# First mixer of a two-block transformer: matrices of a pair of heads kept compactly instead of as blocks on a diagonal

## The chip, the cores and the metric

The kernel runs on one core of a Trainium2 chip. The metric is device time in microseconds (us), the median of several runs. The five engines are TensorE (PE in the profile, with its weight loads as PEld), VectorE (DVE), ScalarE (ACT), GpSimd (POOL) and SyncE (SP), whose queue issues nearly all DMA.

## The reference

Two transformer blocks on 256 tokens of width 1024, batch 1. The change lies in the RWKV half of the first block's mixer: 8 heads of 64, a recurrence over the tokens with a state of 64x64 for each head.

```python
def step(state, inp):
    r_t, k_t, v_t, w_t, a_t, b_t = inp
    sa = jnp.einsum('bhvk,bhk->bhv', state, a_t)
    state = state * w_t[:, :, None, :] + sa[..., None] * b_t[:, :, None, :] + v_t[..., None] * k_t[:, :, None, :]
    return state, jnp.einsum('bhvk,bhk->bhv', state, r_t)
...
ret = jax.nn.silu(rp[..., 3 * RET_WIDTH:]) * ret.reshape(B, S, RET_WIDTH)
rw = rwkv7_time_mix(proj[..., 4 * RET_WIDTH:], rwkv_mu[l], ...)
mixed = jnp.concatenate([ret, rw], axis=-1).astype(x.dtype)
h = h + mixed @ w_out[l]
h = h + hier_moe(rms_norm(h, norm2_gain[l]), ...)
```

After the mixer follow 32 experts of which each token uses two, then a second block (attention and a large product-key layer).

## The kernel before

The first mixer is a set of Python generators (features, four pairs of heads in `rwkv`, retention, output projection) that `interleave` runs by turns while the program is built: each `yield` names a number, the TensorE time that is to pass before the generator goes on. The sum of that time is kept in `self.pe` (`mm` adds an estimate for every product, `tr` a fixed one). So the order of every engine's instructions is fixed when the program is built, and each engine works its own list in that order.

`rwkv(p, ...)` treats heads 2p and 2p+1 together, on partitions 0 to 63 and 64 to 127, with the 256 tokens in 4 chunks of 64. For each chunk it builds a 64x64 triangular matrix (`NB[:, :, 0]`, a unit matrix with the products of `bbd` and `ar` above it), and inverts it in five levels of doubling: `X` holds the inverse so far and `XT` its transpose. A level is a block of products NB·X, an operation on VectorE that masks it into `Z`, and a block of products Z·XT and XT·Z, from which `X` and `XT` are copied again. Then come `UU` (inverse times right-hand sides), `G` and `Q`, and a chain over the chunks whose state is `Sb`.

Every matrix that serves as the stationary operand is kept as [128, ..., 128] with the two heads as blocks on a diagonal and zeros elsewhere. So a product for one head runs over all 128 rows and writes 64 columns (`128*64` in the profile), the two heads' products follow each other, and whatever writes such a matrix needs one operation for each head:

```python
for h in range(2):
    nc.vector.tensor_tensor(Z[col(h), :, col(h)], b[col(h)],
                            mlev[col(h), k][:, None, :].to_broadcast([64, 4, 64]), OP.mult)
```

The products of the features and of the output projection (`u,xt`, `xt,u`, `u,mix` in the profile) use weights split into two parts by ScalarE (L214) and VectorE (L221); their blocks stand between the small ones. The expert stage reads 192 chunks of 1 MB (`in_wB`) into places that are reused: SyncE issues a load when the products on the old content are done, the first ones into memory that the mixer gives up (`first_experts`, `prefetch`, L911).

Of the kernel before, what the change touches and what calls it, by code (L numbers as in the profile page):

```python
# [21 lines left out]
S, D = 256, 1024  # L22
# [8 lines left out]
def shape_constants():  # L31
    f = np.float32
    p = np.arange(128)
    q = p % 64
    c64 = np.arange(64)
    parts = {}
# [4 lines left out]
    lv = []  # L41
    for k in range(6):
        b = 1 << k
        t, s = q[:, None], c64[None, :]
# [10 lines left out]
    n = 0  # L55
# [17 lines left out]
    t = np.arange(S, dtype=np.float64)  # L73
# [92 lines left out]
class K:  # L166
# [375 lines left out]
    def rwkv_setup(self):  # L542
        nc = self.nc
        zs = {}
        E = lambda shape, tag, dt=F32, **k: self.t(self.ap["first"], shape, dt, tag, **k)
        for tag, shape, n in (("sg", [128, 4, 65], 2), ("tl", [128, 2, S], 1), ("bbd", [128, 4, 128], 1), ("kbd", [128, 4, 128], 1),
                              ("NB", [128, 4, 2, 128], 2), ("nka", [128, 4, 128], 1), ("nkr", [128, 4, 128], 2),
                              ("Z", [128, 4, 128], 2), ("Sb", [128, 3, 128], 2)):
            zs[tag] = [self.t(self.ap["even" if tag == "Z" else ("even", "odd")[j] if tag in ("NB", "nkr", "Sb") else "first"], shape, F32, f"{tag}_{j}_") for j in range(n)]
            for z in zs[tag]:  # L550
                nc.gpsimd.memset(z, 0.0)
        zs["tl"] = zs["tl"][0]
        zs["gs"] = E([128, S], "gs")
        zs["h0"] = E([128, 8], "h0")
        o, _ = VEC["rwkv_w0"]
        nc.vector.tensor_scalar(zs["h0"], self.vec[:, o:o + 8], 0.5, None, op0=OP.mult)
        zs["fe"] = [E([128, 257], f"fe_{b}_") for b in range(2)]
        for f in zs["fe"]:
            nc.vector.memset(f[:, 0:1], 0.0)
        zs["smask"] = E([128, 4, 65], "smask")  # L560
        nc.gpsimd.memset(zs["smask"], 1.0)
        nc.gpsimd.memset(zs["smask"][:, :, 0:1], 0.0)
        for z in zs["NB"]:
            nc.gpsimd.tensor_copy(z[:, :, 0], self.ident[:, None, :].to_broadcast([128, 4, 128]))
        return zs

    def rwkv(self, p, zs, lora, gup):

        nc = self.nc
# [5 lines left out]
        ones2, ident, ident2 = self.c("ones2"), self.ident, self.c("ident2")  # L575
# [7 lines left out]
        sg, bbd, kbd, NB, nka, nkr, Z, Sb = (zs[k][p % len(zs[k])] for k in ("sg", "bbd", "kbd", "NB", "nka", "nkr", "Z", "Sb"))  # L583
# [71 lines left out]
        for src in (bbd, kbd):  # L655
            b = self.bank([128, 4, 2, 64])
            for c in range(4):
                for h in range(2):
                    mm(b[col(h), c].rearrange("p a t -> p (a t)"), src[:, c, col(h)],
                       ar[:, c].rearrange("p a t -> p (a t)"), start=True, stop=True)  # L660
            for h in range(2):
                bc = lambda z: z[:, None, :].to_broadcast([64, 4, 64])
# [10 lines left out]
        for c in range(4):  # L673
            for j, f in enumerate((ar[:, c, 0], w4(vp)[:, c])):
                for h in range(2):
                    mm(b[col(h), j, c], f, ident[:, col(h)], start=True, stop=True)
        nc.scalar.activation(rhs[:, :, 0], b[:, 0], AF.Copy)
        nc.scalar.activation(vt, b[:, 1], AF.Copy)
        bT = T([128, 4, 128], "bT")
        kT = T([128, 4, 128], "kT")  # L680
        for src, dst in ((bbd, bT), (kbd, kT)):
            b = self.bank([128, 4, 128])
# [6 lines left out]
        for c in range(4):  # L689
            for h in range(2):  # L690
                mm(b[col(h), c], nka[:, c, col(h)], vt[:, c], start=True, stop=True)
# [5 lines left out]
        XT = T([128, 4, 128], "XT")  # L697
        nc.gpsimd.tensor_tensor(XT, NB[:, :, 0], mt0[:, None, :].to_broadcast([128, 4, 128]), OP.mult)
        b = self.bank([128, 4, 64])
        for c in range(4):  # L700
            for h in range(2):
                mm(b[col(h), c], NB[:, c, 0, col(h)], ident2, start=True, stop=True)
        nc.vector.tensor_tensor(X, b, mlev[:, 0][:, None, :].to_broadcast([128, 4, 64]), OP.mult)
        for k in range(1, 6):
            yield 1.0
            b = self.bank([128, 4, 64])
            for c in range(4):
                for h in range(2):
                    mm(b[col(h), c], NB[:, c, 0, col(h)], X[:, c], start=True, stop=True)
            for h in range(2):  # L710
                nc.vector.tensor_tensor(Z[col(h), :, col(h)], b[col(h)],
                                        mlev[col(h), k][:, None, :].to_broadcast([64, 4, 64]), OP.mult)
            yield 1.2
            b = self.bank([128, 2, 4, 64])
            for c in range(4):
                for h in range(2):
                    mm(b[col(h), 1, c], Z[:, c, col(h)], XT[:, c, col(h)], start=True, stop=True)
                if k < 5:
                    for h in range(2):
                        mm(b[col(h), 0, c], XT[:, c, col(h)], Z[:, c, col(h)], start=True, stop=True)  # L720
# [9 lines left out]
        for c in range(4):  # L730
            for h in range(2):
                mm(b[col(h), c], XT[:, c, col(h)], rhs[:, c].rearrange("p a t -> p (a t)"), start=True, stop=True)
# [3 lines left out]
        for c in range(4):  # L736
            if c < 3:
                for h in range(2):
                    mm(b[col(h), 0, c], UU[:, c, 0], bT[:, c, col(h)], start=True, stop=True)
            for h in range(2):  # L740
                mm(b[col(h), 1, c], UU[:, c, 0], NB[:, c, 1, col(h)], start=True, stop=True)
# [3 lines left out]
        nc.vector.tensor_tensor(Q, b[:, 1], ar[:, :, 1], OP.add)  # L745
        for c in range(3):
            yield 1.75
            b = self.bank([128, 64])
            terms = [(bT[:, c], UU[:, c, 1], True), (kT[:, c], vt[:, c], True)]
            if c:  # L750
                terms.append((G[:, c], Sb[:, c - 1], False))
            self.col_sums(b, terms)
            for h in range(2):
                nc.vector.tensor_scalar(Sb[col(h), c, col(h)], b[col(h)], gam[col(h), c:c + 1], None, op0=OP.mult)
# [3 lines left out]
        for c in range(4):  # L758
            terms = [(NB[:, c, 1], UU[:, c, 1], True), (nkr[:, c], vt[:, c], True)]
            if c:  # L760
                terms.append((Q[:, c], Sb[:, c - 1], False))
            self.col_sums(b[:, c], terms)
# [14 lines left out]
        for c in range(4):  # L777
            for h in range(2):
                mm(b[col(h), c], y[:, c], ident[:, col(h)], start=True, stop=True)
# [12 lines left out]

    def col_sums(self, out, terms):

        for n, (l, r, left) in enumerate(terms):
            for h in range(2):
                hs = slice(64 * h, 64 * h + 64)
                self.mm(out[hs], l[:, hs] if left else l, r if left else r[:, hs],
                                      start=n == 0, stop=n == len(terms) - 1, skip_group_check=True)
# [1091 lines left out]
```

## Time and profile before

| | |
|---|---|
| median of 3 runs | 1655.43 us (1652.95 to 1655.73) |
| profiled execution, its own time | 1654.47 us |
| its span, first to last instruction | 1652.7 us |
| busy share of TensorE, VectorE, ScalarE, GpSimd | 96%, 60%, 40%, 14% |
| stretch of the RWKV matrices | about 40 to 205 us |
| expert stage, DMA | about 256 to 700 us at 407 GB/s |

Shares over the span are means over very different stages. Matmuls are pipelined: their bars overlap, and idle time of TensorE is counted from the modelled end of the last one.

### The profile page before, as it was taken

The numbers are of one execution on the slowest core, as the hardware profiler recorded it, in microseconds if no ns is written. First come the engines' busy times: TensorE is split into PE (matmuls) and PEld (weight loads), VectorE is DVE, ScalarE is ACT, GpSimd is POOL, SyncE is SP. The second block draws the span as 40 slices with busy tenths as digits, with TensorE's granted clock in tenths as the row PEclk, the third lists the DMA queues.
The fourth block names the chain that finished last, engine by engine and source line by source line (L and its number), as shares of the span: only waits on it lengthen the run. The fifth ranks groups of instructions, "written<-read, shape, count | busy, mean of one in ns | idle before, by whom it ended". The sixth has DMA issues, their size and how long they took to land.

```text
span 1652.7 us, 27958 instructions
## 1 busy us (share of the span) xinstructions
PE 1590.4 (96%) x11022; PEld 1223.9 (74%) x11022; DVE 997.4 (60%) x1917; ACT 658.5 (40%) x1175; POOL 233.2 (14%) x264
## 2 busy tenths in 40 slices
PE   7998999999999998899999999999999999999998
PEld 7787784534443343367889999999999888888887
DVE  6878662212121211288979988788899755555554
ACT  5333341211121111155655456555544444444443
POOL 5212120000000000066110000123445100000000
PEclk9999999999999999999999999999999999999999
DMA  6222688999999999964255556555555566666664
GB/s 202 91 65 65 225 359 348 415 389 419 420 419 420 420 419 420 370 194 136 82 181 174 182 179 193 166 166 166 167 160 163 166 195 195 193 192 193 194 197 155
DMA packets 84296, 390.63 MB, mean 236 GB/s; under 512 B 9632, under 2 KB 9776, under 8 KB 63424
## 3 DMA queue, kind: packets, MB, share of 16 engines
q1 hardware_dynamic: 83088, 384.48, 65.2%
q0 software_dynamic: 928, 3.25, 0.6%
q8 instruction: 89, 1.46, 0.4%
q10 hardware_dynamic: 144, 1.05, 0.2%
q14 instruction: 47, 0.39, 0.1%
HBM read 386.65 MB, written 2.10 MB: 235 GB/s over the span
## 4 chain that ended last, share of the span: by engine, by line
PE 53%; DVE 2%; POOL 2%; issue 1%; ACT 0%; ACTq 0%; DVEq 0%; POOLq 0%
PE b L255 52%; POOL rs_r L341 1%; DVE u L221 1%; PE b L267 1%; DVE g L1748 0%; POOL rs_m L339 0%; POOL y L1439 0%; POOL rs_r L1428 0%; DVE oh L1856 0%; ACT s L1472 0%; DVE h L472 0%; DVE u L1705 0%; DVE ss L1426 0%; DVE qz L1451 0%; DVE mx L1468 0%
## 5 line engine op out<-in xcount | busy, mean ns | idle before, releaser
L214 ACT ACTIVATE u<-u 128x1024 fp32r<-128x1024 f32 x334 | 354.2, 1061 | 387.0 <-PE b L255 363.9
L221 DVE TENSOR_TENSOR u<-u,u 128x1024 fp32r<-128x1024 f32 x334 | 412.9, 1237 | 148.4 <-PE b L255 115.1
L255 PE MATMUL b<-mix,u 128*128 128x256 f32 x3456 | 425.6, 281 | 0.0
L255 PEld LDWEIGHTS b<-mix,u 128*128 128x128 f32 x3456 | 411.1, 188 | 0.0
L255 PE MATMUL b<-u,oh 128*128 128x512 f32 x1536 | 350.3, 390 | 2.0 <-ACT oh L1688 2.0
L255 PEld LDWEIGHTS b<-u,oh 128*128 128x128 f32 x1536 | 289.3, 188 | 62.8 <-ACT oh L1688 2.2
L255 PE MATMUL b<-mr,u 128*64 128x512 f32 x944 | 231.2, 595 | 17.3 <-DMA mr<-in_wB 17.2
L255 PEld LDWEIGHTS b<-mr,u 128*64 128x64 f32 x944 | 74.5, 137 | 157.1 <-issue 119.0
L1151 DVE TENSOR_TENSOR hh<-hh,b 128x512 f32<-128x512 f32 x16 | 11.0, 687 | 230.2 <-PE b L255 230.2
L1732 POOL TENSOR_TENSOR g<-g,gelu 128x4 f32<-128x4 f32 (+43 forms) x87 | 94.3, 1084 | 355.1 <-ACT gelu L1731 348.1
L255 PE MATMUL b<-u,xt 128*128 128x512 f32 x480 | 124.6, 410 | 0.8 <-DVE u L221 0.8
L255 PE MATMUL b<-mr,hT 128*64 128x512 f32 x480 | 117.5, 603 | 5.5 <-DVEq L1215 2.4
L255 PEld LDWEIGHTS b<-u,xt 128*128 128x128 f32 x480 | 89.9, 192 | 21.6 <-DVE u L221 1.1
L1196 DVE SCALAR_TENSOR_TENSOR u<-b,sw,u 128x512 fp32r<-128x512 f32 x32 | 23.9, 750 | 133.3 <-ACT u L1195 133.3
L255 PEld LDWEIGHTS b<-mr,hT 128*64 128x64 f32 x480 | 35.9, 138 | 74.6 <-issue 69.7
L1176 ACT ACTIVATE hT<-b 128x512 f32<-128x512 f32 x16 | 9.6, 597 | 159.6 <-PE b L267 159.6
L1689 DVE TENSOR_TENSOR oh<-g,oh 128x512 fp32r<-128x512 f32 x64 | 44.3, 693 | 41.0 <-ACT oh L1688 40.9
L1324 POOL MEMSET qz<- 128x2048 f32 x2 | 3.5, 1799 | 451.0 <-DVEq L1215 451.0
L1195 ACT ACTIVATE u<-b,sw 128x512 fp32r<-128x512 f32 x32 | 21.9, 687 | 109.0 <-PE b L255 109.0
L1748 DVE TENSOR_TENSOR g<-g,b 128x252 f32<-128x252 f32 (+47 forms) x111 | 61.5, 592 | 0.0
L1856 DVE TENSOR_TENSOR oh<-oh,gw 128x512 f16<-128x512 f16 x128 | 54.4, 464 | 0.0
L255 PE MATMUL b<-xt,u 128*128 128x256 f32 x336 | 47.7, 297 | 3.9 <-DVE u L221 2.3
(390 smaller groups left out, 1736.6 us busy)
## 6 DMA issues: line engine op xcount, KB each, us to landing
mr<-in_wB SPq DMA_DIRECT2D x160, 1024.0 KB, 15.9
u<-in_down SPq DMA_DIRECT2D x128, 512.0 KB, 3.6
u<-in_up SPq DMA_DIRECT2D x128, 512.0 KB, 3.5
mr<-in_wB SPq DMA_DIRECT2D x36, 512.0 KB, 15.0
u<-in_wA SPq DMA_DIRECT2D x30, 512.0 KB, 3.7
u<-in_wB SPq DMA_DIRECT2D x28, 512.0 KB, 13.5
u<-in_wC SPq DMA_DIRECT2D x24, 512.0 KB, 4.4
u<-in_wQ SPq DMA_DIRECT2D x16, 512.0 KB, 3.6
```

Of the source, the lines that this page charges most:

```text
L214: nc.scalar.activation(hi, r, AF.Copy)
L221: nc.vector.tensor_tensor(lo, r, hi.bitcast(F32), OP.subtract)
L255: self.nc.tensor.matmul(out, l, r, start=start, stop=stop, **k)
L267: self.nc.tensor.transpose(out, x, self.ident)
L341: nc.gpsimd.tensor_tensor(r, m, self.mhalf[:, :width], OP.pow)
L1151: nc.vector.tensor_tensor(self.hh, self.hh, bs[1], OP.mult)
L1195: nc.scalar.activation(yh[:, o], b, AF.Copy, scale=sw)
L1196: nc.vector.scalar_tensor_tensor(yl[:, o], b, sw, yh[:, o].bitcast(F32), op0=OP.mult, op1=OP.subtract)
L1689: nc.vector.tensor_tensor(lo, src, hi.bitcast(F32), OP.subtract)
L1732: nc.gpsimd.tensor_tensor(dst[:, 0:n], dst[:, 0:n], g[:, 0:n], OP.mult)
L1748: nc.vector.tensor_tensor(d, d, s, OP.mult)
L1856: self.nc.vector.tensor_tensor(w[:, :, part].rearrange("p t (k x) -> p t k x", x=2), o[:, :, 0].rearrange("p t (k x) -> p t k x", x=2), se ...
```

## The change

`NB`, `nka`, `nkr`, `Z`, `XT`, `Sb` and the former `bbd`, `kbd`, `bT`, `kT` (now `bd`, `kd` and the halves of `bkT`) become [128, ..., 64], a head on 64 partitions. A helper `heads` issues the two products of a pair, each over 64 rows and 64 columns; every write of such a matrix is one operation over 128 partitions. `XT` is copied by ScalarE alone. The transposes of `bbd` and `kbd` (`tr`, 128x128) become products with a 64-row identity. The zeroing of the old matrices by GpSimd goes, and within a level the product that becomes `X` is issued ahead of that which becomes `XT`. Places in memory move, since the tiles are smaller.

```diff
-        for tag, shape, n in (("sg", [128, 4, 65], 2), ("tl", [128, 2, S], 1), ("bbd", [128, 4, 128], 1), ("kbd", [128, 4, 128], 1),
-                              ("NB", [128, 4, 2, 128], 2), ("nka", [128, 4, 128], 1), ("nkr", [128, 4, 128], 2),
-                              ("Z", [128, 4, 128], 2), ("Sb", [128, 3, 128], 2)):
...
+        for tag, shape, n in (("sg", [128, 4, 65], 2), ("tl", [128, 2, S], 1), ("NB", [128, 4, 2, 64], 2)):
...
+        def heads(out, l, r, start=True, stop=True):
+            for h in range(2):
+                mm(out[col(h)], l[col(h)], r[col(h)], start=start, stop=stop, skip_group_check=not (start and stop))
...
-        for h in range(2):
-            nc.vector.tensor_tensor(bbd[col(h), :, col(h)], w4(kr)[col(h)], e3p[col(h)], OP.mult)
-            nc.gpsimd.tensor_tensor(kbd[col(h), :, col(h)], w4(k2)[col(h)], e3p[col(h)], OP.mult)
+        bd, kd = E([128, 4, 64], "bd"), E([128, 4, 64], "kd")
+        nc.vector.tensor_tensor(bd, w4(kr), e3p, OP.mult)
+        nc.gpsimd.tensor_tensor(kd, w4(k2), e3p, OP.mult)
...
-                if src is bbd:
-                    nc.vector.copy_predicated(NB[col(h), :, 0, col(h)], bc(mtri[col(h), 0].bitcast(I32)), b[col(h), :, 0])
-                    nc.vector.tensor_tensor(NB[col(h), :, 1, col(h)], b[col(h), :, 1], bc(mtri[col(h), 1]), OP.mult)
-                else:
-                    nc.vector.tensor_tensor(nka[col(h), :, col(h)], b[col(h), :, 0], bc(mtri[col(h), 0]), OP.mult)
-                    nc.vector.tensor_tensor(nkr[col(h), :, col(h)], b[col(h), :, 1], bc(mtri[col(h), 1]), OP.mult)
+                heads(b[:, c].rearrange("p a t -> p (a t)"), src[:, c], ar[:, c].rearrange("p a t -> p (a t)"))
+            if src is bd:
+                nc.vector.copy_predicated(NB[:, :, 0], bc(0).bitcast(I32), b[:, :, 0])
+                nc.vector.tensor_tensor(NB[:, :, 1], b[:, :, 1], bc(1), OP.mult)
+            else:
+                nc.vector.tensor_tensor(nka, b[:, :, 0], bc(0), OP.mult)
+                nc.vector.tensor_tensor(nkr, b[:, :, 1], bc(1), OP.mult)
...
-                self.tr(b[:, c], src[:, c])
-            nc.scalar.activation(dst, b, AF.Copy)
+                heads(b[:, j, c], src[:, c], ident2)
+        nc.scalar.activation(bkT, b, AF.Copy)
...
-            for h in range(2):
-                nc.vector.tensor_tensor(Z[col(h), :, col(h)], b[col(h)],
-                                        mlev[col(h), k][:, None, :].to_broadcast([64, 4, 64]), OP.mult)
+            nc.vector.tensor_tensor(Z, b, lev(k), OP.mult)
...
-            nc.vector.tensor_copy(XT[col(0), :, col(0)], b[col(0), 1])
-            nc.scalar.activation(XT[col(1), :, col(1)], b[col(1), 1], AF.Copy)
+            nc.scalar.activation(XT, b[:, 1], AF.Copy)
...
-            for h in range(2):
-                nc.vector.tensor_scalar(Sb[col(h), c, col(h)], b[col(h)], gam[col(h), c:c + 1], None, op0=OP.mult)
+            nc.vector.tensor_scalar(Sb[:, c], b, gam[:, c:c + 1], None, op0=OP.mult)
```

What this does to the lists of the engines is seen at three places. The first is VectorE's list at about 45 to 49 us, where the products of `bbd` and `kbd` for the first pair of heads are masked into `NB`, `nka` and `nkr`. Before:

```order
L221 TENSOR_TENSOR u_539<-u_369,u_501 128x1024
L664 COPY_PREDICATED NB_44_222<-cst_80,b_568 64x4x64
L665 TENSOR_TENSOR NB_44_222<-b_568,cst_80 64x4x64
L664 COPY_PREDICATED NB_44_222<-cst_80,b_568 64x4x64
L665 TENSOR_TENSOR NB_44_222<-b_568,cst_80 64x4x64
L667 TENSOR_TENSOR nka_46_226<-b_581,cst_80 64x4x64
L668 TENSOR_TENSOR nkr_47_228<-b_581,cst_80 64x4x64
L667 TENSOR_TENSOR nka_46_226<-b_581,cst_80 64x4x64
L668 TENSOR_TENSOR nkr_47_228<-b_581,cst_80 64x4x64
L528 TENSOR_TENSOR fe_55_243<-b_543,R_280 128x256
```

Now:

```order
L218 TENSOR_TENSOR u_519<-u_349,u_481 128x1024
L663 COPY_PREDICATED NB_42_218<-cst_80,b_550 128x4x64
L664 TENSOR_TENSOR NB_42_218<-b_550,cst_80 128x4x64
L666 TENSOR_TENSOR nka_548<-b_561,cst_80 128x256
L667 TENSOR_TENSOR nkr_549<-b_561,cst_80 128x256
L525 TENSOR_TENSOR fe_46_223<-b_523,R_260 128x256
```

Eight operations on 64 partitions became four on 128; the neighbours are the same. The second place is TensorE's list at about 71 to 73 us, the end of the same step for the second pair, where `cst` is the identity and `X,NB` a level of the first pair. Before:

```order
L255 MATMUL b_918<-cst_72,ft_632 64x64 x2
L267 MATMUL b_939<-cst_72,bbd_42_218 128x128 x4
L267 MATMUL b_945<-cst_72,kbd_43_220 128x128 x4
L255 MATMUL b_951<-X_669,NB_44_222 64x64 x8
L255 MATMUL b_739<-u_634,xt_13_133 128x512
```

Now:

```order
L252 MATMUL b_894<-cst_80,ft_615 64x64 x2
L252 MATMUL b_914<-cst_80,bd_782 64x64 x8
L252 MATMUL b_914<-cst_80,kd_783 64x64 x8
L252 MATMUL b_932<-X_652,NB_42_218 64x64 x8
L252 MATMUL b_722<-u_617,xt_13_133 128x512
```

Eight transposes of 128x128 became sixteen products of 64x64, and nothing stands elsewhere. The third place is VectorE's list at about 121 to 129 us, ahead of a state `Sb` of the second pair for which TensorE waits. Before:

```order
L754 TENSOR_SCALAR Sb_52_237<-b_1567,gam_697 64x64 x2
L528 TENSOR_TENSOR fe_55_243<-b_1458,R_280 128x256
L530 TENSOR_TENSOR d_1575<-fe_55_243 128x256
L532 SCALAR_TENSOR_TENSOR ft_1577<-d_1575,vec_83,fe_55_243 128x256
L221 TENSOR_TENSOR u_1581<-u_1189,u_1452 128x1024
L636 TENSOR_SCALAR ri_1598<-b_1595 128x256
L637 RECIPROCAL ri_1598<-ri_1598 128x256
L640 SCALAR_TENSOR_TENSOR ar_1601<-kr_1539,e_1514 128x4x64
L642 TENSOR_TENSOR ri_1598<-ri_1598,av_1496 128x256
L643 TENSOR_TENSOR kr_1539<-kr_1539,ri_1598 128x256
L645 TENSOR_TENSOR bbd_42_218<-kr_1539,e_1515 64x4x64 x2
L754 TENSOR_SCALAR Sb_52_237<-b_1610,gam_697 64x64 x2
```

Now:

```order
L745 TENSOR_SCALAR Sb_1503<-b_1534,gam_681 128x64
L525 TENSOR_TENSOR fe_46_223<-b_1424,R_260 128x256
L527 TENSOR_TENSOR d_1541<-fe_46_223 128x256
L529 SCALAR_TENSOR_TENSOR ft_1543<-d_1541,vec_83,fe_46_223 128x256
L218 TENSOR_TENSOR u_1547<-u_1164,u_1418 128x1024
L637 TENSOR_SCALAR ri_1564<-b_1561 128x256
L638 RECIPROCAL ri_1564<-ri_1564 128x256
L641 SCALAR_TENSOR_TENSOR ar_1567<-kr_1506,e_1480 128x4x64
L643 TENSOR_TENSOR ri_1564<-ri_1564,av_1462 128x256
L644 TENSOR_TENSOR kr_1506<-kr_1506,ri_1564 128x256
L646 TENSOR_TENSOR bd_1572<-kr_1506,e_1481 128x256
L745 TENSOR_SCALAR Sb_1503<-b_1576,gam_681 128x64
```

The order is the same; the two `Sb` and the `bbd` are each one operation for two.

## Rows read from the trace of the kernel before

**Rows 1.** Busy time by stretch: start:end, length, each engine busy (instructions), clock, DMA.

```profile
40.00:70.00 30.00, 26.50 (x346) 21.97 (x347) 28.57 (x58) 10.50 (x22) 9.45 (x8) 1.00 0.29 90
70.00:112.00 42.00, 38.89 (x636) 34.44 (x632) 29.68 (x65) 13.56 (x26) 6.35 (x8) 0.99 0.24 75
112.00:150.00 38.00, 34.17 (x395) 28.39 (x394) 30.28 (x71) 13.10 (x28) 7.80 (x10) 0.87 0.18 58
150.00:185.00 35.00, 31.71 (x606) 27.06 (x606) 27.74 (x63) 11.43 (x27) 11.23 (x13) 1.00 0.49 175
185.00:256.00 71.00, 70.04 (x540) 58.22 (x538) 47.44 (x99) 27.21 (x40) 14.04 (x25) 1.00 0.80 311
256.00:700.00 444.00, 422.05 (x2031) 180.92 (x2030) 81.95 (x165) 71.52 (x141) 0.00 (x0) 1.00 0.99 407
```

**Rows 2.** Waits of TensorE, 0 to 280 us: total, times, longest.

```profile
PE b L255 <- DVE Z L711: 5.4, 8, 2.5
...
PE b L255 <- DVE Sb L754: 2.5, 1, 2.5
...
PE b L255 <- DVE nka L667: 2.1, 4, 0.9
...
PE b L255 <- DVE X L703: 1.9, 3, 1.0
```

**Rows 3.** VectorE groups by form, 0 to 280 us: busy, mean ns, idle before.

```profile
L711 DVE TENSOR_TENSOR Z<-b,cst 64x256 f32<-64x256 f32 x40 | 16.8, 420 | 2.7 <-PE b L255 1.9
...
L723 DVE COPY XT<-b 64x256 f32<-64x256 f32 x20 | 8.3, 415 | 12.2 <-ACT X L722 11.2 <-PE b L255 0.8
...
L664 DVE COPY_PREDICATED NB<-cst,b 64x256 f32<-64x256 int32 x8 | 3.6, 447 | 0.1
...
L703 DVE TENSOR_TENSOR X<-b,cst 128x256 f32<-128x256 f32 x4 | 1.7, 418 | 0.0
```

**Rows 4.** VectorE in order of time, 104 to 110 us: start, length, [idle before].

```profile
104.86 0.43 DVE L774 TENSOR_TENSOR y<-y,rs_r 128x256 f32<-128x256 f32 x1 [1.45 <-POOL rs_r L341]
...
109.03 0.87 DVE L711 TENSOR_TENSOR Z<-b,cst 64x256 f32<-64x256 f32 x2
```

**Rows 5.** TensorE in order of time, 104 to 110 us.

```profile
109.49 0.33 PE L255 MATMUL b<-XT,Z 128*64 128x64 f32 x2 [2.55 <-DVE Z L711]
```

**Rows 6.** VectorE in order of time, 124 to 130 us.

```profile
124.99 1.75 DVE L637 RECIPROCAL ri<-ri 128x256 f32<-128x256 f32 x1
...
127.92 0.85 DVE L645 TENSOR_TENSOR bbd<-kr,e 64x256 f32<-64x256 f32 x2
...
128.80 0.60 DVE L754 TENSOR_SCALAR Sb<-b,gam 64x64 f32<-64x64 f32 x2
```

**Rows 7.** TensorE in order of time, 71 to 75 us.

```profile
71.56 0.66 PE L267 MATMUL b<-cst,bbd 128*128 128x128 f32 x4
...
72.59 0.69 PE L255 MATMUL b<-X,NB 128*64 128x64 f32 x16
...
73.20 1.66 PE L255 MATMUL b<-u,xt 128*128 128x512 f32 x6
```

**Rows 8.** TensorE in order of time, 129 to 133 us.

```profile
129.86 2.93 PE L255 MATMUL b<-u,xt 128*128 128x512 f32 x6
```

**Rows 9.** TensorE matmuls by form, 0 to 280 us (19 such forms, the most and the fewest).

```profile
L255 PE MATMUL b<-XT,Z 128*64 128x64 f32 x320 | 21.9, 226 | 6.2 <-DVE Z L711 5.4 <-ACT qT L822 0.2
...
L255 PE MATMUL b<-Sb,G 128*64 128x64 f32 x32 | 2.9, 237 | 2.5 <-DVE Sb L754 2.5
```

**Rows 10.** ScalarE group by form, 0 to 280 us.

```profile
L724 ACT ACTIVATE XT<-b 64x256 f32<-64x256 f32 x20 | 7.6, 379 | 33.2 <-DVE XT L723 33.2
```

**Rows 11.** SyncE queue in order of time, 244 to 294 us.

```profile
245.07 2.48 SPq L911 DMA_DIRECT2D u<-in_wB  x2
258.26 35.35 SPq L911 DMA_DIRECT2D mr<-in_wB  x16
```

**Rows 12.** Waits of the SyncE queue, 256 to 700 us.

```profile
SPq L911 <- DMA mr<-in_wB: 245.3, 129, 3.0
```

More of the change, by code (lines that the diff above doesn't have):

```diff
@@ L582, in rwkv @@
         tl, gs = zs["tl"], zs["gs"]
-        sg, bbd, kbd, NB, nka, nkr, Z, Sb = (zs[k][p % len(zs[k])] for k in ("sg", "bbd", "kbd", "NB", "nka", "nkr", "Z", "Sb"))
+        sg, NB = (zs[k][p % 2] for k in ("sg", "NB"))
+        def heads(out, l, r, start=True, stop=True):
+            for h in range(2):
+                mm(out[col(h)], l[col(h)], r[col(h)], start=start, stop=stop, skip_group_check=not (start and stop))
         if p == 0:
@@ L654, in rwkv @@
         yield 5.0
[L655 removed]
+        nka, nkr = E([128, 4, 64], "nka"), T([128, 4, 64], "nkr")
+        bc = lambda n: mtri[:, n, None, :].to_broadcast([128, 4, 64])
+        for src in (bd, kd):
             b = self.bank([128, 4, 2, 64])
             for c in range(4):
[L658 to L668 removed]
+                heads(b[:, c].rearrange("p a t -> p (a t)"), src[:, c], ar[:, c].rearrange("p a t -> p (a t)"))
[5 more added lines that the diff above has]
+                nc.vector.tensor_tensor(nkr, b[:, :, 1], bc(1), OP.mult)
         rhs = T([128, 4, 2, 64], "rhs")
@@ L674, in rwkv @@
             for j, f in enumerate((ar[:, c, 0], w4(vp)[:, c])):
-                for h in range(2):
-                    mm(b[col(h), j, c], f, ident[:, col(h)], start=True, stop=True)
+                heads(b[:, j, c], f, ident2)
         nc.scalar.activation(rhs[:, :, 0], b[:, 0], AF.Copy)
         nc.scalar.activation(vt, b[:, 1], AF.Copy)
[L679 to L682, printed above, removed]
+        bkT = T([128, 2, 4, 64], "bkT")
+        bT, kT = bkT[:, 0], bkT[:, 1]
+        b = self.bank([128, 2, 4, 64])
+        for j, src in enumerate((bd, kd)):
             for c in range(4):
-                self.tr(b[:, c], src[:, c])
-            nc.scalar.activation(dst, b, AF.Copy)
+                heads(b[:, j, c], src[:, c], ident2)
+        nc.scalar.activation(bkT, b, AF.Copy)
         yield 1.75
@@ L689, in rwkv @@
         for c in range(4):
-            for h in range(2):
-                mm(b[col(h), c], nka[:, c, col(h)], vt[:, c], start=True, stop=True)
+            heads(b[:, c], nka[:, c], vt[:, c])
         nc.scalar.activation(rhs[:, :, 1], b, AF.Copy)
@@ L696, in rwkv @@
         X = T([128, 4, 64], "X")
-        XT = T([128, 4, 128], "XT")
-        nc.gpsimd.tensor_tensor(XT, NB[:, :, 0], mt0[:, None, :].to_broadcast([128, 4, 128]), OP.mult)
+        XT = T([128, 4, 64], "XT")
+        Z = T([128, 4, 64], "Z")
+        lev = lambda k: mlev[:, k, None, :].to_broadcast([128, 4, 64])
+        nc.gpsimd.tensor_tensor(XT, NB[:, :, 0], mt0[:, None, :].to_broadcast([128, 4, 64]), OP.mult)
         b = self.bank([128, 4, 64])
         for c in range(4):
-            for h in range(2):
-                mm(b[col(h), c], NB[:, c, 0, col(h)], ident2, start=True, stop=True)
-        nc.vector.tensor_tensor(X, b, mlev[:, 0][:, None, :].to_broadcast([128, 4, 64]), OP.mult)
+            heads(b[:, c], NB[:, c, 0], ident2)
+        nc.vector.tensor_tensor(X, b, lev(0), OP.mult)
         for k in range(1, 6):
@@ L707, in rwkv @@
             for c in range(4):
-                for h in range(2):
-                    mm(b[col(h), c], NB[:, c, 0, col(h)], X[:, c], start=True, stop=True)
-            for h in range(2):
-                nc.vector.tensor_tensor(Z[col(h), :, col(h)], b[col(h)],
-                                        mlev[col(h), k][:, None, :].to_broadcast([64, 4, 64]), OP.mult)
+                heads(b[:, c], NB[:, c, 0], X[:, c])
+            nc.vector.tensor_tensor(Z, b, lev(k), OP.mult)
             yield 1.2
@@ L730, in rwkv @@
         for c in range(4):
-            for h in range(2):
-                mm(b[col(h), c], XT[:, c, col(h)], rhs[:, c].rearrange("p a t -> p (a t)"), start=True, stop=True)
+            heads(b[:, c], XT[:, c], rhs[:, c].rearrange("p a t -> p (a t)"))
         nc.scalar.activation(UU.rearrange("p c a t -> p c (a t)"), b, AF.Copy)
@@ L737, in rwkv @@
             if c < 3:
[L738 to L741, printed above, removed]
+                heads(b[:, 0, c], UU[:, c, 0], bT[:, c])
+            heads(b[:, 1, c], UU[:, c, 0], NB[:, c, 1])
         G = T([128, 3, 64], "G")
@@ L745, in rwkv, with sums @@
         nc.vector.tensor_tensor(Q, b[:, 1], ar[:, :, 1], OP.add)
+        Sb = T([128, 3, 64], "Sb")
+        def sums(out, terms):
+            for n, (l, r) in enumerate(terms):
+                heads(out, l, r, n == 0, n == len(terms) - 1)
         for c in range(3):
@@ L758, in rwkv @@
         for c in range(4):
[L759 to L762, printed above, removed]
+            sums(b[:, c], [(NB[:, c, 1], UU[:, c, 1]), (nkr[:, c], vt[:, c])] + ([(Q[:, c], Sb[:, c - 1])] if c else []))
         self.done.add(("out", p))
@@ L777, in rwkv @@
         for c in range(4):
-            for h in range(2):
-                mm(b[col(h), c], y[:, c], ident[:, col(h)], start=True, stop=True)
+            heads(b[:, c], y[:, c], ident2)
         o = L([128, S], "y2")
@@ L791, in mid @@
         return m[:, :, None].to_broadcast([128, 4, 65])
[L793 to L799, printed above, removed]
     def ret_turn(self, rot, rt, g):
```

27 lines of the change are left out of this document (10 added, 17 removed).

## The prediction

> **What bounds the kernel now.** I read the busy time by stretch first, to see which engine each stretch rests on. From 40 to 185 us, where the matrices of the heads are worked, TensorE is busy 131.3 of 145 us; its idle time is 3.5, 3.1, 3.8 and 3.3 us in the four stretches, 13.7 us together. VectorE is busy nearly as long, 28.6 of the first 30 us [rows 1]. From 185 to 256 us TensorE is busy 70.0 of 71 us. Then come 444 us of experts in which DMA is busy 0.99 of the time [rows 1].
>
> The list of TensorE's waits says what that idle time is: 5.4 us for `Z`, 2.5 for one `Sb`, 2.1 for `nka`, 1.9 for `X`, 16 waits and 11.9 us [rows 2]. All four are written by VectorE, and all four by operations that the change halves or that queue behind such. Idle time counts from the end of the last matmul, and a small one is 0.226 us long [rows 9] while 16 of them start within 0.61 us [rows 7], 0.038 us apart. So each wait costs some 0.19 us more than its idle time, 3.0 us for the 16.
>
> The groups of VectorE show why halving helps: `Z` for one head, on 64 partitions, takes 420 ns; `X`, as many columns on 128 partitions, takes 418 ns [rows 3]. An operation costs by its columns. Two halves of 420 ns become one of about 420.
>
> **Does a gain up to 185 us reach the end?** TensorE has 1 us idle from 185 to 256 us, so that stretch moves as a whole. The expert loads are what is left: SyncE issues one at 245 to 247.5 us and then none until 258.26, when the first products on expert weights have freed a place [rows 11]. All places are full by then, so the DMA stream starts with those products, and from then on it is the limit (SyncE waited 245.3 us for earlier loads to land [rows 12]). The expert stage moves with its first product, to the microsecond.
>
> **The change part by part.**
>
> *VectorE.* For each of four pairs 18 operations go: 5 halves of `Z`, 5 copies of `XT`, 4 of the NB, nka and nkr masks, 1 of `bbd`, 3 of `Sb`. At 420, 415, 447 ns and about 300 for `Sb` [rows 3, 6] that is 20 x 0.42 + 20 x 0.415 + 20 x 0.42 + 12 x 0.3 = 28.7 us of work. It is not the gain: the gain is what TensorE waited, place by place.
>
> - 40 to 70 us: idle 3.5 us, with five waits. VectorE's queue is full, and ahead of the last wait 11 operations go (2 `bbd`, 4 masks, 3 `Z`, 2 `XT`), 4.6 us. That is more than the waits and their 0.9 us of run-out. I take 4.0, since `X` is still a short chain of product, mask, product.
> - 70 to 112 us: idle 3.1 us, of which 2.55 is one wait for `Z`, at 109.49 [rows 5]. VectorE began afresh at 104.86, after a wait for GpSimd [rows 4], and between it and `Z` stand mostly operations that stay. Gone are one `XT` and the second half of `Z`: 0.85 us. With two small waits (0.6 us) 1.5.
> - 112 to 150 us: idle 3.8 us. The wait for `Sb`, 2.5 us, stands behind a reciprocal of 1.75 us that stays; half of `bbd` and of two `Sb` go [rows 6]: 0.43 + 0.3 + 0.1 = 0.8 us. The rest, for `X` and `Z`, stands behind the eight masks, now four (1.7 us): 1.3. Together 2.1.
> - 150 to 185 us: idle 3.3 us in many small waits, some ten, with 1.9 us of run-out. Two pairs run through their levels at once and 20 operations go, 8 us. Besides, VectorE's copy of `XT` waited 11.2 us for ScalarE's `X` in the whole mixer, at the head of its queue [rows 3]; that goes too. What stays is the chain of a level. I take 4.0.
>
> Sum: 4.0 + 1.5 + 2.1 + 4.0 = 11.6 us.
>
> *The clock.* From 112 to 150 us the granted clock was 0.87 [rows 1], so 2 x 0.13 x 38 = 9.9 us were at 1.2 GHz, the rest at 2.4. It fell after the two long waits. Six products `u,xt` took 2.93 us then and 1.66 us at the full clock [rows 7, 8], 43% of the time lost: up to 4.3 us in all. The long waits shrink only to 1.7 or 2 us, so it may fall again; part of the loss was hidden by VectorE. I take 1.5, with 0 and 4.3 as ends.
>
> *ScalarE.* It now copies all of `XT` behind `X`, 0.38 us as its half does now [rows 10]. Before, that half waited 33.2 us in total for VectorE's half [rows 10]. `X` comes first and `XT` is read only after the next `Z`, so a copy of 0.38 us lies beside a block of products and a mask. If that cover failed in all 20 levels, 7.6 us.
>
> *TensorE.* The products keep their number and columns; rows fall from 128 to 64. No row shows a product of 64 rows. Below: a block of 16 takes 0.61 us as now [rows 7]; with fewer rows to run through it may be a little quicker to end. Above: the two heads no longer run together. Now they do: a product of 64 columns is 0.226 us long [rows 9] and starts come 0.038 us apart. One at a time the 1,824 small products of the 19 forms [rows 9] would start at least twice as far apart: 1,824 x 0.033 = 60 us more. I take nothing, because the two heads write the same partitions of a bank as now, and only their inputs sit on other rows.
>
> The Trainium skill, TensorEngine Tiling (Array Packing), section Restrictions and Gotchas, says that different row tiles can't use one PSUM bank at the same time and that software has to keep them apart. Here both heads of `b` lie in one bank. The trace has only column tiles, which do share a bank, so it neither bears the rule out nor refutes it for rows; by the rule the heads would go one after the other, and that is the rival "one at a time" below.
>
> The 8 transposes of a pair take 1.03 us [rows 7] (71.56 to 72.59); 32 small matmuls at 0.03 to 0.038 take 1.0 to 1.2. Nothing, or 0.8 us for four pairs.
>
> *GpSimd and memory.* The zeroing of old matrices goes; nothing in TensorE's waits comes from it [rows 2]. If anything waited, it would be the first `NB`. Places move, and the first expert loads wait for other operations; DMA is busy 0.80 of 71 us there [rows 1], so 14 us are free to make up a late load.
>
> Sum: 11.6 + 1.5 = 13.1. The profiled execution took 1654.47 us, so 1641.4; the median of before is 1.0 above that execution, so **1642 us**.
>
> **Rivals.**
>
> - *Forecast* (0.58), 1637 to 1647.
> - *All waits go and the clock holds* (0.13): 13.7 + 4.8 of run-out (25 waits) + 4.3 = 22.8 at the very most; at 85% of it 19.5: 1636. For it: VectorE loses twice the work that was waited for. Against: the two longest waits sit behind operations that stay.
> - *The wait moves to ScalarE* (0.12): XT uncovered, 13.1 - 6 = 7: 1648. Against: XT is needed one block and one mask after X.
> - *The stage of experts doesn't move* (0.06): its loads become the bound from 185 us on, because the new places come free later. 1655. Against it the 14 us above.
> - *One at a time* (0.07), slower: in every block of a mixer level. A block of 16 would take 1.2 us instead of 0.61. There are 1,824 / 16 = 114 such blocks, so the gain of 13 us is used up when a block takes 0.11 us longer, 0.72. Fully, + 60 - 13: 1702. For it: no row of 64-row products. Against: same banks, same partitions.
> - *The clock falls more often* (0.04), slower: half the rows work in a small product. 26 us more at 1.2 GHz would use up the gain; half of the 145 us would give 1655 + 36 - 12 = 1679. For it: the clock fell here twice. Against: at 160 to 185 us, dense in small products, it was 1.00 [rows 1].
>
> **How the numbers follow.** 0.2% of the time is 3.3 us, about what a measurement here can tell from none. Faster by more: the first three, 0.83. Within it: the fourth and a rest of the slower two, 0.07. Slower: 0.10. The range holds the first three, from 1634 to 1651 us, and leaves out the others and the tails of these.
>
> **What would show it.** `Z` 20 times on 128 partitions at 0.42 us, no `XT` on VectorE; waits for `nka` and `X` gone, for `Z` under 3 us, for `Sb` near 1.7; blocks of 16 small products within 0.6 us; the first load after the pause at about 245 us instead of 258.26; from there the same length to the end. I am wrong if blocks take longer, if TensorE waits for `XT`, or if the pause of the loads shrinks while the later loads stay where they were.

## The result and the profile after

The changed kernel takes 1638.46 us (median of four) against 1655.33 us for the kernel before (also of four): a ratio of 0.9892, with a 95% interval from 0.9869 to 0.9915. One of the four, which took 3164 us, counts in that median but not in the ratio; the other three took 1633.89 to 1638.77. That is 17 us gained where 13 were forecast. The profiled execution took 1633.89 us, with a span of 1632.1; before it was 1654.47 and 1652.7.

Busy time by stretch, the same stretches as in [rows 1] (start:end, length, PE, PEld, DVE, ACT, POOL, clock, DMA share, GB/s):

```profile
40.00:70.00 30.00, 29.99 (x502) 25.45 (x500) 23.69 (x46) 11.64 (x26) 9.05 (x8) 1.00 0.34 107
70.00:112.00 42.00, 39.37 (x591) 35.30 (x587) 24.38 (x52) 13.30 (x27) 4.90 (x7) 0.92 0.25 77
112.00:150.00 38.00, 35.84 (x528) 29.75 (x529) 32.30 (x68) 12.78 (x27) 10.38 (x13) 1.00 0.22 71
150.00:185.00 35.00, 33.59 (x629) 28.58 (x625) 15.99 (x35) 11.47 (x24) 7.28 (x12) 1.00 0.72 265
185.00:256.00 71.00, 69.16 (x425) 51.00 (x424) 40.70 (x92) 25.49 (x37) 12.20 (x22) 1.00 0.80 304
256.00:700.00 444.00, 422.75 (x2040) 184.22 (x2041) 90.14 (x168) 78.63 (x153) 9.18 (x7) 1.00 0.99 407
```

In the first stretch TensorE is no longer idle at all, and VectorE has 6 us free where it had 1.4. A stretch now holds more of the program than before, since everything comes sooner; that is why VectorE looks busier from 112 to 150 us.

The waits of TensorE from 40 to 185 us (total, times, longest):

```profile
PE b L252 <- DVE Z L707: 3.4, 3, 2.6
PE b L252 <- DVE Sb L745: 1.4, 1, 1.4
PE b L252 <- issue: 0.6, 2, 0.4
PE b L252 <- ACT X L715: 0.3, 1, 0.3
PE b L252 <- ACT rhs L724: 0.2, 1, 0.2
```

The four kinds of wait of [rows 2] had 11.9 us in 16 waits; 4.8 us in four are left. Those for `nka` and for VectorE's `X` are gone. The two long ones that are left are the two of which the prediction said that they stand behind operations that stay. `Z` has 3.4 us in all, where the prediction expected less than 3. The first one, seen on both engines (start, length, [idle before]):

```profile
97.43 0.43 DVE L762 TENSOR_TENSOR y<-y,rs_r 128x256 f32<-128x256 f32 x1 [1.45 <-POOL rs_r L338]
...
101.28 0.41 DVE L707 TENSOR_TENSOR Z<-b,cst 128x256 f32<-128x256 f32 x1
...
101.84 1.12 PE L252 MATMUL b<-XT,Z 64*64 64x64 f32 x16 [2.63 <-DVE Z L707]
```

VectorE still stands 1.45 us for GpSimd's root. `Z` ends 4.26 us after the start of the `y` that was held up; before, its second half ended after 5.04 [rows 4], 0.78 us later (0.85 was forecast). But TensorE had begun before that, 0.04 us after the first half, 4.63 us after `y` [rows 5]; now it begins 4.41 us after `y`, and it comes to the place 0.3 us sooner. So its idle time there didn't shrink: 2.63 us against 2.55.

The groups of VectorE and of ScalarE by form (busy, mean ns, idle before), to be held against [rows 3, 10]:

```profile
L707 DVE TENSOR_TENSOR Z<-b,cst 128x256 f32<-128x256 f32 x20 | 8.4, 420 | 10.5 <-PE b L252 10.4
...
L745 DVE TENSOR_SCALAR Sb<-b,gam 128x64 f32<-128x64 f32 x12 | 3.4, 280 | 4.9 <-PE b L252 4.9
...
L663 DVE COPY_PREDICATED NB<-cst,b 128x256 f32<-128x256 int32 x4 | 1.8, 442 | 0.9 <-PE b L252 0.9
```

```profile
L716 ACT ACTIVATE XT<-b 128x256 f32<-128x256 f32 x20 | 7.6, 378 | 11.5 <-PE b L252 11.5
```

`Z` on 128 partitions takes the 420 ns that its half took. And it is now VectorE that waits for products ahead of `Z`, 10.4 us in all, where it waited 1.9 before: its queue runs empty at these places. ScalarE's copy of all of `XT` takes 378 ns, as the half did.

The products by form (heads on 64 rows, busy and mean ns), against [rows 9], and one block of 16 against [rows 7]:

```profile
L252 PE MATMUL b<-XT,Z 64*64 64x64 f32 x320 | 18.9, 224 | 2.6 <-DVE Z L707 2.6
...
L252 PE MATMUL b<-Sb,G 64*64 64x64 f32 x32 | 2.3, 221 | 1.4 <-DVE Sb L745 1.4
```

```profile
47.95 0.68 PE L252 MATMUL b<-X,NB 64*64 64x64 f32 x16
```

A product of 64 rows takes 224 ns against 226, a block 0.68 us against 0.69. And the queue of loads, for [rows 11]:

```profile
230.19 2.19 SPq L890 DMA_DIRECT2D u<-in_wB  x2
243.10 18.18 SPq L890 DMA_DIRECT2D mr<-in_wB  x9
```

The pause ends at 243.10 instead of 258.26: 15.2 us of the gain are there when the experts begin.

### The profile page after: what moved, and what is told of

Same layout as the page of the kernel before. It is cut to its first block, busy times and chain, and to the rows that moved or that the text cites. A ratio compares the mean times of both kernels' runs of the same rounds, so it can differ in the third digit from the quotient of the medians.

```text
span 1632.1 us, 28041 instructions
## 1 busy us (share of the span) xinstructions
PE 1581.5 (97%) x11118; PEld 1217.2 (75%) x11118; DVE 967.6 (59%) x1845; ACT 654.9 (40%) x1171; POOL 218.8 (13%) x249
## 4 chain that ended last, share of the span: by engine, by line
PE 53%; DVE 2%; POOL 2%; issue 1%; ACT 0%; ACTq 0%; DVEq 0%; POOLq 0%
PE b L252 53%; POOL rs_r L338 1%; DVE u L218 1%; PE b L264 1%; DVE g L1727 0%; POOL rs_m L336 0%; POOL y L1418 0%; POOL rs_r L1407 0%; DVE oh L1835 0%; ACT s L1451 0%; DVE h L469 0%; DVE u L1684 0%; DVE ss L1405 0%; DVE qz L1430 0%; DVE mx L1447 0%
## 5 line engine op out<-in xcount | busy, mean ns | idle before, releaser
L1129 ACT ACTIVATE hh<-b 128x512 f32<-128x512 f32 x16 | 9.6, 597 | 99.3 <-PE b L252 99.3
## 6 DMA issues: line engine op xcount, KB each, us to landing
mr<-in_wB SPq DMA_DIRECT2D x160, 1024.0 KB, 15.2
```

## The experiments

Each run is given as a ratio to the kernel before, timed beside it on the same chip. The base is the changed kernel once more, run with the first three experiments (a0): 1637.57 us against 1653.92, ratio 0.9903 [0.9888, 0.9917]. "Above a0" is the difference of the ratios, with 1655 us for 1; it is uncertain by some 3 us, and by over 4 for the runs with the wider intervals.

> The changed kernel once more, as the base of the runs beside it. Its profiled execution (1633.9 us) was the shortest of three (1638.2 and 1638.8 were the others). Expected 1634 to 1640. If the 4.5 us between executions come from the stage of experts, the pause of the loads ends near 243 us again and the rest of the span differs; if from the start (the granted clock in the first 20 us), the pause ends up to 2 us later.

It was 1637.57, as expected. The profiled execution had a span 3.6 us longer than the first one of the changed kernel, and neither of the two guesses on the cause was right: the granted clock was 0.93 from 185 to 256 us, in the router, where it had been 1.00, and the pause of the loads ended at 246.83 instead of 243.10. The start was slower too (0.91 from 0 to 40 us), but by 183 us the two traces stand even again, 15.1 and 15.2 us ahead of the kernel before. The first stretch of the first trace of the changed kernel, and then the first and the router's of a0:

```profile
0.00:40.00 40.00, 32.32 (x228) 30.11 (x230) 27.35 (x55) 20.82 (x35) 11.82 (x29) 1.00 0.64 208
```

```profile
0.00:40.00 40.00, 31.57 (x211) 29.74 (x212) 26.51 (x52) 21.04 (x35) 11.31 (x28) 0.91 0.63 207
185.00:256.00 71.00, 70.17 (x413) 54.32 (x413) 40.22 (x91) 25.49 (x37) 12.22 (x22) 0.93 0.75 281
```

### All operations on two heads in halves again

```diff
-            nc.vector.tensor_tensor(Z, b, lev(k), OP.mult)
+            for h in range(2):
+                nc.vector.tensor_tensor(Z[col(h)], b[col(h)], mlev[col(h), k][:, None, :].to_broadcast([64, 4, 64]), OP.mult)
...
-            nc.scalar.activation(XT, b[:, 1], AF.Copy)
+            nc.vector.tensor_copy(XT[col(0)], b[col(0), 1])
+            nc.scalar.activation(XT[col(1)], b[col(1), 1], AF.Copy)
```

and likewise the masks, `bd` and `Sb`. The matrices stay compact, the products stay at 64 rows.

> The changed kernel with its 64-row products, but every VectorE operation on two heads done as two of 64 partitions again (Z, masks, bd, Sb), and XT half by VectorE, half by ScalarE: 72 operations, some 28.7 us, back on VectorE. Theory (VectorE's queue is the whole gain): TensorE's waits come back, 11 us of them and perhaps 2 of clock, so 10 to 15 us above a0, 1646 to 1653. Rival (the gain lies in products of 64 rows, transposes, memory, or the zeroing that went): within 3 us of a0.

1648.52 us, ratio 0.997 [0.9957, 0.9983]: 11 us above a0, in the theory's range and far from the rival's. TensorE's four largest waits from 40 to 185 us in this run:

```profile
PE b L252 <- DVE Z L711: 5.6, 9, 2.6
PE b L252 <- DVE Sb L751: 2.6, 1, 2.6
PE b L252 <- DVE nka L669: 2.2, 4, 0.8
PE b L252 <- DVE X L704: 1.9, 3, 1.0
```

These are the rows of the kernel before [rows 2], nearly number by number (5.4, 2.5, 2.1, 1.9), though every product of the heads is on 64 rows. So VectorE's operations make these waits, and 11 of the 17 us. But the run is still 5 us faster than the kernel before: something else in the change, or in how it stands in the program, gives that.

### One part in halves at a time

The same edits, for `XT` alone, for `Z` alone, for both, and for the masks, `bd` and `Sb` alone.

> The changed kernel with the lower half of XT copied by VectorE again (20 operations, 8.3 us, which wait at the head of the queue for ScalarE's X). Theory: by its share of the operations (20 of 72) and since it blocks the queue, 3 to 5 us above a0. Rival (XT on ScalarE alone lies on the path, so sharing it pays): up to 3 us below a0. Rival (rows, not VectorE): no difference.

> The changed kernel with Z in two operations of 64 partitions (20 more, 8.4 us). Theory: these stand between two blocks of products of a level, so they cost more than their share: 4 to 7 us above a0. Rival (other products of TensorE cover the chain of a level): under 2 us.

> The changed kernel with NB, nka, nkr, bd and Sb in two operations of 64 partitions again (32 more, some 12 us; Z and XT stay single). XT's half and Z's half alone cost nothing that could be measured, all parts together 11 us. Theory (each part has a price of its own, and the dear one is this: it stands ahead of the waits for nka, X and Sb): 6 to 10 us above a0, 1644 to 1648. Rival (VectorE's queue has room for any one part; only when all come back does it fill up): under 3 us above a0.

> The changed kernel with both Z and XT in halves (40 operations, 16.7 us on VectorE). Theory (a price for each part): the sum of the two alone, -1 and +1.5, so within 2 us of a0. Rival (the queue fills up): more than the sum, 3 to 8 us above a0.

| run | ratio to the kernel before | above a0, us | TensorE's waits, 40 to 185 us |
|---|---|---|---|
| changed kernel (0.9903 is a0, the waits are of its first trace) | 0.9903 [0.9888, 0.9917] | 0 | 5.9 |
| XT in halves | 0.9887 [0.9872, 0.9903] | -2.6 | 7.2 |
| Z in halves | 0.9922 [0.9908, 0.9936] | 3.1 | 6.3 |
| both | 0.9916 [0.9898, 0.9933] | 2.2 | 8.9 |
| masks, bd and Sb in halves | 0.993 [0.9906, 0.9954] | 4.5 | 11.2 |
| all | 0.997 [0.9957, 0.9983] | 11.1 | 14.2 |

The last column is the sum of all listed waits of one trace (before: 13.1), and finer than the times. It counts the `issue` waits, in which TensorE waited for nothing that the profile shows: 0.6 us in the changed kernel and 2.0 with the masks, `bd` and `Sb` in halves, where one alone took 1.8; none in the other traces of the table. Nothing ties them to VectorE, so the parts are compared without them here, against the 5.3 us that the changed kernel then has. My prices were too high: for `XT` (3 to 5) the time shows no loss and the waits 1.9 us, for `Z` (4 to 7) the waits show 1.0, while its time, 3.1, is too uncertain to decide. The time of `XT` alone, 2.6 us below a0, doesn't exclude the rival that sharing the copy pays, but TensorE's list has no wait for `XT` that sharing could take away. Together the two make 3.6, a little more than the sum of 2.9, as a queue that fills up would do; one trace of each and the times are too coarse to tell. The masks, `bd` and `Sb` make 3.9 us of waits, hardly more than those two, and the waits that come back are those of `nka`, `X` and `Sb`:

```profile
PE b L252 <- DVE Z L710: 3.1, 3, 2.6
PE b L252 <- DVE Sb L749: 2.7, 2, 2.4
PE b L252 <- issue: 2.0, 2, 1.8
PE b L252 <- DVE X L704: 1.6, 2, 1.0
PE b L252 <- DVE nka L669: 1.3, 3, 0.8
```

3.9 and 3.6 make 7.5 of the 8.9 us by which the waits of "all" exceed those of the changed kernel. In time the masks, `bd` and `Sb` fell short of the 6 to 10 us that I gave them, though the interval reaches to 9. Which part is the dear one is therefore not shown; that all of them together carry 11 us is.

### The two heads one after the other

The products of a block are issued for all of head 0 first and then, by a call of `second()` behind each block, for all of head 1.

```diff
-            for h in range(2):
-                mm(out[col(h)], l[col(h)], r[col(h)], start=start, stop=stop, skip_group_check=not (start and stop))
+            h = 0
+            mm(out[col(h)], l[col(h)], r[col(h)], start=start, stop=stop, skip_group_check=not (start and stop))
+            late.append((out, l, r, start, stop))
+
+        def second():
+            for out, l, r, start, stop in late:
+                h = 1
+                mm(out[col(h)], l[col(h)], r[col(h)], start=start, stop=stop, skip_group_check=not (start and stop))
+            late.clear()
```

> The changed kernel with the products of a block issued head by head: all of the first head, then all of the second, so that two neighbours never lie on different quarters of the array. Theory (the two heads of a pair run together in the changed kernel, on their own rows and columns): now each of 16 products starts 0.05 to 0.06 us after the last instead of 0.03, a block takes 0.9 to 1.0 us instead of 0.61, and with 110 blocks the kernel is 30 to 50 us above a0, 1668 to 1688. Rival (they went one at a time already): within 5 us of a0.

1666.13 us, ratio 1.0068 [1.0046, 1.009]: 27 us above a0, a little under the theory's 30 to 50 and far from the rival. A block of this run:

```profile
52.04 0.96 PE L252 MATMUL b<-X,NB 64*64 64x64 f32 x16
```

0.96 us instead of 0.68, so with 114 blocks 32 us; 3.0 us of that come back, because TensorE's waits fall from 5.9 to 2.9 us when it is slower. So in the changed kernel the heads do run together. The first records of a block, cut off 12 ns after the first start in the changed kernel and 62 ns after it in this run, show it directly:

```profile
47.95 0.27 PE L252 MATMUL b<-X,NB 64*64 64x64 f32 x2
```

```profile
52.04 0.27 PE L252 MATMUL b<-X,NB 64*64 64x64 f32 x1
```

In the changed kernel the two heads start 7 ns apart, and the next pair as a rule 58 ns later; in this run the records of one head are 58 ns apart too. But even here the heads are not wholly one after the other: head 1 starts at 52.325 us, when three of head 0's eight records have yet to start (52.378, 52.436 and 52.494). Strictly in sequence, head 1 would start 0.23 us later and a block would take some 1.19 us (an estimate from these starts).

Both heads lie in one bank of PSUM, on different rows of the array, which the Trainium skill, TensorEngine Tiling (Array Packing), section Restrictions and Gotchas, says can't be at the same time; for two heads that write different partitions of the bank, this trace and this run don't agree with it.

### Two small parts

The products of a level in the old order, and GpSimd's zeroing put back on a tile that nobody reads:

```diff
-                if k < 5:
-                    heads(b[:, 0, c], XT[:, c], Z[:, c])
                 heads(b[:, 1, c], Z[:, c], XT[:, c])
+                if k < 5:
+                    heads(b[:, 0, c], XT[:, c], Z[:, c])
```

```diff
+        zero = self.t(self.ap["first"], [128, 1024], F32, "zero")
+        for n in (512, 512, 1024, 1024, 512, 512, 512, 512, 512, 384, 384):
+            nc.gpsimd.memset(zero[:, 0:n], 0.0)
```

> The changed kernel with the two products of a level in the old order: the one that becomes XT ahead of the one that becomes X, ScalarE's copies as now. Theory (the chain of a level goes through X, but a block of 16 lasts 0.6 us and other products fill the wait): within 1.5 us of a0. Rival (the order carries part of the gain): 2 to 5 us above a0.

> The changed kernel with GpSimd's zeroing put back at its place in the list, on a tile that nobody reads, in the old sizes (6.5 us of GpSimd between 18 and 25 us). Theory (no wait of TensorE comes from it): within 1.5 us of a0, and TensorE's first RWKV products at the same time. Rival (the unit matrices of NB and what follows on GpSimd come later and hold the first pair): 2 to 5 us above a0, all of it before 50 us.

Old order 0.9893 [0.9871, 0.9916], zeroing 0.9889 [0.9868, 0.9911]: no difference from a0 that these runs could tell, to some 4 us. The waits for `Z` and `Sb` are those of a0 in both traces (3.4 and 1.4 us). So neither carries the main part of the gain.

### Where the other five microseconds are

From the first expert product to the end the kernel should have stayed rigid, but the changed one was 3.5 to 3.9 us shorter there, around 700 us, in all the first five traces with compact matrices. That is the end of the expert stage, where TensorE's program goes on behind a branch. The kernel before, in its first trace and in a second one (b0):

```profile
700.72 0.61 PE L255 MATMUL b<-mr,hT 128*64 128x512 f32 x1 [2.42 <-DVEq L1215]
702.59 5.06 PE L255 MATMUL b<-mr,hT 128*64 128x512 f32 x15 [1.26 <-issue]
```

```profile
699.98 0.61 PE L255 MATMUL b<-mr,hT 128*64 128x512 f32 x1 [2.42 <-DVEq L1215]
702.12 6.58 PE L255 MATMUL b<-mr,hT 128*64 128x512 f32 x15 [1.53 <-issue]
```

The changed kernel there:

```profile
683.39 3.65 PE L252 MATMUL b<-mr,hT 128*64 128x512 f32 x16 [1.78 <-DVEq L1194]
```

Before, one record runs, TensorE stands 1.3 to 1.5 us for nothing that the profile shows, and the other 15 run in part at half clock (granted clock 0.71 and 0.50 over the 5.06 us from 702.59). After, 16 run without a break, in 3.65 us. The all-halves run has no stall here either. In its trace it was, besides, 3.4 us ahead of the kernel before when the experts began (first product at 252.88 against 256.26): 1.4 of that were there at 16 us, and the clock fell less from 112 to 150 us (0.96 against 0.87). So the stall explains the larger part of the five microseconds, and differences of the clock in single traces can hide or add the rest. The changed kernel issues 96 more matmul records ahead of this place. To see whether that matters, the kernel before got 96 small products on constants at its very start:

```diff
             self.warm(WARM[0], self.cst2[:, 0:128])
+            b = self.bank([128, 64])
+            for _ in range(96):
+                nc.tensor.matmul(b[0:64], self.cst2[0:64, 0:64], self.cst2[0:64, 64:128], start=True, stop=True)
```

> The kernel before once more, for a second trace. In its first trace TensorE stood for 1.3 us at 701 us, at the end of the stage of experts, and worked at half clock after it, about 3.7 us in all, which none of the traces with compact matrices shows. If that was chance, it is absent here and the span from the pause of the loads to the end is 3 to 4 us shorter than in the first trace; if it belongs to the program, it stands here again. The waits between 40 and 185 us should be the same to 0.5 us.

> The kernel before, with 96 products of 64x64 on constants put at its very start, where TensorE waits for the input: as many as the changed kernel issues more. Both traces of the kernel before show TensorE standing 1.3 to 1.5 us after one product at 700 us, for nothing that the profile shows, and the clock falling after it (some 3.5 us); none of eight traces with compact matrices does. Theory (how many instructions stand ahead of that place decides, since it shifts where TensorE's list is cut): the stall at 700 us is gone, the span from the first expert product on is 3 to 4 us shorter, the whole 0 to 4 us below the kernel before. Rival (it comes from the places in memory or from the products themselves): the stall stands as before, and the time is within 2 us of it.

The second trace of before (an execution of 1657.27 us) has the stall too, so it wasn't chance; and with the products ahead it is gone:

```profile
4.81 12.04 PE L334 MATMUL b<-cst 64*64 64x64 f32 x192
...
707.52 3.65 PE L255 MATMUL b<-mr,hT 128*64 128x512 f32 x16 [2.41 <-DVEq L1218]
```

The run itself was slower, 1658.98 us, ratio 1.0025 [1.0006, 1.0045], slower than either theory expected (though the interval reaches down to 1 us), because the products took 12 us and held the first transposes of the input. By TensorE's start of the same products, this run was 6.6 us behind the first trace of before at 603 us and 3.5 us behind it at 708 us: 3.1 us came back at the stall. The trace counts two records for each product, so 192 and not 96 were added; this shows that products put ahead can remove the stall without any change in the matrices, and not that just this number did so in the changed kernel. They also moved the place by 6.8 us in time, so the count of instructions and the moment aren't told apart.

### A version that is faster than both

Two operations leave VectorE: the product of `y` with its root goes to GpSimd, which makes the root, and `Sb` goes to ScalarE.

```diff
-            nc.vector.tensor_scalar(Sb[:, c], b, gam[:, c:c + 1], None, op0=OP.mult)
+            nc.scalar.activation(Sb[:, c], b, AF.Copy, scale=gam[:, c:c + 1])
...
-        nc.vector.tensor_tensor(y, y, r[:, :, None].to_broadcast([128, 4, 64]), OP.mult)
+        nc.gpsimd.tensor_tensor(y, y, r[:, :, None].to_broadcast([128, 4, 64]), OP.mult)
```

> The changed kernel with two operations moved off VectorE: the product of y with its reciprocal root goes to GpSimd, which makes the root (VectorE waits for it 1.45 us at the head of its queue ahead of the one long wait for Z), and Sb goes to ScalarE (the one wait for Sb stands behind a reciprocal of 1.75 us). Theory (what is left of TensorE's waits is these two chains): the wait for Z falls from 2.6 to under 1 us, that for Sb from 1.4 to under 0.5, the granted clock doesn't fall at 101 us; 3 to 6 us below a0. Rival (GpSimd's slower operation or ScalarE's queue makes a new wait): within 1 us, or slower.

1630.84 us, ratio 0.9861 [0.9841, 0.9881]: 7 us below a0 (3 to 6 were expected, and the figure is uncertain by 4), the fastest of all. Its waits, and two of its stretches:

```profile
PE b L252 <- DVE Z L707: 2.1, 3, 1.3
PE b L252 <- ACT X L715: 0.3, 1, 0.3
PE b L252 <- ACT rhs L724: 0.2, 1, 0.2
```

```profile
70.00:112.00 42.00, 40.67 (x653) 36.59 (x649) 26.86 (x55) 17.26 (x36) 8.06 (x10) 1.00 0.25 77
112.00:150.00 38.00, 37.34 (x663) 31.70 (x663) 29.50 (x60) 13.09 (x30) 11.94 (x14) 1.00 0.29 91
```

The wait for `Sb` is gone, the long one for `Z` is halved, and the clock stays at 1.00 where it was 0.92: 2 x 0.08 x 42 = 6.7 us at 1.2 GHz that no longer are. The longest wait for `Z` went only to 1.3, not under 1. That the shorter wait is what kept the clock up isn't shown: in the trace with `Z` in halves the wait had its full length and the clock didn't fall either.

```profile
70.00:112.00 42.00, 39.30 (x643) 34.89 (x642) 27.26 (x59) 13.55 (x27) 4.90 (x7) 1.00 0.24 77
```

```profile
104.66 1.04 PE L252 MATMUL b<-XT,Z 64*64 64x64 f32 x16 [2.63 <-DVE Z L708]
```

## Why the prediction was right, point by point

The time (1638.46) lies in the range, 3.5 us below the forecast.

**VectorE's queue is where the gain is.** Right: putting its 72 operations back costs 11 us and gives the waits of [rows 2] again. An operation on 128 partitions costs what one on 64 did: `Z` 420 ns.

**The waits place by place, 11.6 us.** Measured where the kernel stands against before, by TensorE's starts of the same product: 2.5 us gained from 25 to 62 us and 4.6 from 25 to 73 (forecast 4.0 for 40 to 70); 0.5 from 73 to 115, with the clock's fall at 101 us in it (1.5); 4.6 from 115 to 147 (2.1 + 1.5 with the clock); 3.6 from 147 to 183 (4.0). Together 13.3 us against 13.1. It isn't so that each of the terms was right: from 73 to 115 us the wait behind `y` didn't shrink at all, since TensorE had started on the first half of `Z` before, and 112 to 150 gave more. The closeness of the sum is in part luck: in the second trace of the changed kernel (a0) the same four places gave 4.6, 1.8, 4.7 and 3.4 us, 14.5 together.

**The clock, 1.5 us.** By stretch, 9.9 us at 1.2 GHz before (from 112 to 150) and 6.7 after (from 70 to 112): it did fall again, after the long wait for `Z`, but not after the 1.4 us wait for `Sb`. Half of the 3.2 us is 1.6. In the second traces of both kernels the two stretches had 7.0 us and 3.4 us at 1.2 GHz together, so the size held. But with `Z` in halves the clock stayed up behind the same wait of 2.63 us: a long wait alone doesn't decide whether it falls.

**ScalarE's XT, at nothing.** Right: TensorE has no wait for `XT` in its list, and halving it again gains nothing that could be measured.

**Products of 64 rows, at nothing.** Right for the time, 224 ns against 226. The rival "one at a time" didn't come. Its price, 60 us, isn't refuted by the 27 us of the run with one head after the other, in which the heads still overlap in part: 0.51 us more for each of 114 blocks, by the estimate of 1.19 us, would be 58. The expected block of "within 0.6 us" was a slip: 0.61 was the distance to the next group's start [rows 7], the block itself took 0.69, and takes 0.68 now. Nor do records start evenly 0.038 us apart: they come in pairs, one of each head, 58 ns from pair to pair.

**Passing rigidly to the end.** Half right. The pause of the loads moved by all of what TensorE had gained up to there, 15.2 us, and the stage of experts behind it came with it. But 1.8 of these 15.2 were there at 25 us already, where the two programs differ little: the granted clock from 0 to 40 us was 0.91 in the trace of before and 1.00 in this one, and the second trace of the changed kernel has 0.91 again. So the trace of the changed kernel that I had was lucky: the second was 1.2 us behind it at 25 us, level with it at 183 us, and 3.7 us behind it again when the experts began. And "the same length to the end" failed: some 4 us were gained at 700 us, at a stall of TensorE that the prediction hadn't looked at. It is this term, at nothing in the sum, by which the forecast was too careful.

What is open: what TensorE waits for at 700 us in the kernel before, and whether the 96 records more are what removed the stall. No run has exactly that number ahead, or the same delay without more records.

## What to carry to other kernels

An engine whose queue is full (28.6 of 30 us here) delays others by all that stands ahead of the operation they wait for, so sum the gain wait by wait and not by the work that goes: 28.7 us less work on VectorE gave 11 us. Waits behind an operation that stays shrink less: the one behind an operation that itself waits at the head of the queue went from 2.55 to 2.63 us, the one behind a reciprocal of 1.75 us from 2.5 to 1.4. Giving two operations to engines with room brought some 7 us more. Look also for stalls far from the change: some 4 of these 17 us came at 700 us, long after the last line touched.

## What the runs showed of the hardware

Two products of 64 rows and 64 columns, one on the lower half of the array's rows and columns and one on the upper, run together though they write one bank (different partitions of it): their records start 7 ns apart, and 16 take 0.68 us when they alternate and 0.96 when they don't.

An operation of VectorE or ScalarE on 128 partitions took as long as one on 64: `Z` 420 ns either way, `XT` 378 and 379.

The granted clock falls in some executions and not in others at the same place in the program: from 0 to 40 us (0.91 in a0, 1.00 in the first trace of the changed kernel) and in the router (0.93 and 1.00). The fall in the router is the 3.7 us by which the pause of the loads ended later in a0, which is the whole difference between these two spans (1632.1 and 1635.7 us). The slower start set a0 back by 1.2 us.
